# The four 32-sample strips of a scan group, one after another or side by side

## The chip, the core and the metric

The kernel runs on one core of one Trainium2 chip. The metric is the device time of one execution, in microseconds (us). The engines that matter here: PE (TensorE, the matrix unit, 128 rows by 128 columns), PEld (its weight loads), DVE (VectorE), ACT (ScalarE), POOL (GpSimd) and SP (which starts the transfers of weights). Each engine works through its own list in order and waits for the others by semaphores.

## The reference, cut to what matters

One layer of a streaming encoder for 256 prompt tokens and 32 sample tokens, 288 in all. The part that changes is the state-space scan (Mamba-2 SSD): 32 heads of 64 channels in 4 groups of 8 heads, state size 128. The prompt is scanned as chunks of the sequence with a state handed on, the sample is one chunk of 32 that starts from a given state.

```python
cum = jnp.cumsum(dtc * a.reshape(B_GROUPS, B_HPG), axis=2)
seg = jnp.where(causal, cum[:, :, :, None] - cum[:, :, None, :], -jnp.inf)
cb = jnp.einsum('bclgn,bcsgn->bclsg', cc, bc)
wgt = cb[..., None] * jnp.exp(seg) * dtc[:, :, None]
y_diag = jnp.einsum('bclsgr,bcsgrp->bclgrp', wgt, x)
decay_to_end = jnp.exp(cum[:, :, -1:] - cum) * dtc
states = jnp.einsum('bclgn,bclgr,bclgrp->bcgrpn', bc, decay_to_end, x)
...
y_off = jnp.einsum('bclgn,bcgrpn,bclgr->bclgrp', cc, h_in, jnp.exp(cum))
```

## The kernel before, in words

All tokens are columns: a tile is 128 channels by 288 tokens. The bulk of the work is the projections. Each projection is cut into jobs; a job is half a strip, a weight block of 8 x 128 x 128 that SP fetches (`wr`), that ACT copies to a rounded half `wh` (L231) and DVE to the rest `wl` (L232), and that PE then uses in 24 matmuls of 288 columns into a bank called `ps` (all matmuls go through the helper at L78). `run` takes one job after another:

```python
        convert()
        go(wh, wl)
        step()
```

`convert` puts the next weight block's copies into the lists of ACT and DVE, `go` the 24 matmuls and, at the end of a strip, the copy of its result, and `step` advances the side work by one `yield`. So in every list the order of one step is: weight copy, result copy, side work. Side work is written as generators; in the scan one is active at a time (`width["n"] = 1`), and when one ends the next starts within the same `step`.

`scan(g)` is the generator of group g. It holds 4 strips of 128 channels (two heads each), and treats the tokens in three column blocks, `COLS`: 0 to 128, 128 to 256 and the 32 samples. Its results on PE go to banks called `sd`; there are five, handed out in turn:

```python
        return psum.tile([P, 512], F32, tag="sd", bufs=5, name="sd")
```

The first matmul into a bank waits until the bank's last reader, five requests earlier, is done. A group asks for 12 banks: `pc`, `pb` (products of C and B, and B transposed), three `px` (the inputs transposed), one for the first state, four for the outputs `po`, two for the later states (`pp`). The work on PE of a group, in its steps: (1) `pc` and `pb`, L914 and L916; (2) `px`, L932, twelve transposes; (3) the first state, one product of 512 columns; (4) and (5) the outputs of two strips each (`out`), where the samples' share is 32 rows by 64 columns of the array; (6) the later states: one product with all 128 rows and one with the samples' 32 rows, 512 columns each. In between DVE subtracts the decays (L950, `decay`), ACT takes exponentials, POOL and DVE multiply by the mask (`mask`, L954; for the samples L982), POOL scales by the decay to the end (L942, `ddx`) and by the whole decay (L1028), and DVE adds the new states (L1031). The samples' tiles use 32 of the 128 partitions.

`g_misc` runs once, early: it makes `dt`, the running sums `cum`, the decays `dde` and `ecE`, and writes the transposed sums to `scr` in memory, from which POOL's transfers (L906, L909) spread them over partitions for each group. The scan runs beside 32 jobs of gate projections (`N_G`), 16 of `pm` and 16 of `az`; after these 64 jobs `begin_y` empties the side work before the next projection goes on.

Of the kernel before, what the change touches and what calls it, by code (L numbers as in the profile page):

```python
# [7 lines left out]
F32 = mybir.dt.float32  # L8
F32R = mybir.dt.float32r
AF = mybir.ActivationFunctionType  # L10
OP = mybir.AluOpType
AX = mybir.AxisListType

P = 128
TP = 256
TS = 32
T = TP + TS
# [5 lines left out]
COLS = ((0, 128, 128), (128, 256, 128), (256, 288, 32))  # L23
# [10 lines left out]
def step_kernel(ctx, tc, ins, outs):  # L34
    nc = tc.nc
    V, S, G, PE = nc.vector, nc.scalar, nc.gpsimd, nc.tensor
    PS = bass.MemoryType.PSUM

    const = ctx.enter_context(tc.tile_pool(name="const", bufs=1))
# [12 lines left out]
    def sd():  # L52
        return psum.tile([P, 512], F32, tag="sd", bufs=5, name="sd")
# [23 lines left out]
    def mm(out, lhsT, rhs, start=True, stop=True):  # L77
        PE.matmul(out, lhsT, rhs, start=start, stop=stop)  # L78
# [28 lines left out]
    ident = const.tile([P, P], F32, name="ident")  # L107
# [6 lines left out]
    tri = const.tile([P, P], F32, name="tri")  # L114
# [463 lines left out]
    dt = const.tile([P, 96], F32, name="dt")  # L578
    cum = const.tile([P, 96], F32, name="cum")
    ecE = const.tile([P, 96], F32, name="ecE")  # L580
    dde = const.tile([P, 96], F32, name="dde")
    scr = dram.tile([32, T], F32, name="scr")

    def g_misc():
        yield
        p = sd()
        for i in range(3):
            PE.transpose(p[:, 64 * i:64 * i + 64], N.mi[64:128, P * i:P * i + P], ident[64:128, 64:128])
        yield
        S.activation(wt, p[:, 0:192].rearrange("p (i c) -> p i c", i=3), AF.Copy)  # L590
        yield
        u, e, z, q, a = (t2(96) for _ in range(5))
        v3 = lambda t: t.rearrange("p (i h) -> p i h", i=3)
        V.tensor_tensor(v3(u), wt[:, :, 32:64], dtb[:, None, :].to_broadcast([P, 3, 32]), OP.add)
        V.tensor_scalar(wt[:, :, 0:16], wt[:, :, 0:16], 1.0 / 32, None, OP.mult)
        for c in range(4):
            V.tensor_copy(ws[32 * c:32 * c + 32], wt[32 * c:32 * c + 32, 2, c:16:4])
        mark("misc")

        V.scalar_tensor_tensor(e, u, -1.0, u, OP.mult, OP.max)  # L600
        S.activation(e, e, AF.Exp, scale=-1.0)
        S.activation(a[:, 0:32], alog, AF.Exp)
        yield
        V.tensor_scalar(z, e, 2.0, None, OP.add)
        V.reciprocal(z, z)
        V.tensor_tensor(z, z, e, OP.mult)
        V.tensor_tensor(q, z, z, OP.mult)
        V.tensor_scalar(e, q, 1.0 / 17, None, OP.mult)
        for n in (15, 13, 11, 9, 7, 5, 3):
            V.scalar_tensor_tensor(e, e, 1.0 / n, q, OP.add, OP.mult)  # L610
        yield
        V.scalar_tensor_tensor(e, e, 1.0, z, OP.add, OP.mult)
        V.tensor_scalar(u, u, 0.0, None, OP.max)
        V.scalar_tensor_tensor(dt, e, 2.0, u, OP.mult, OP.add)
        V.scalar_tensor_tensor(v3(u), v3(dt), -1.0, a[:, None, 0:32].to_broadcast([P, 3, 32]),
                               OP.mult, OP.mult)
        yield
        p = sd()
        for i, (c0, c1, n) in enumerate(COLS):
            h = slice(32 * i, 32 * i + 32)  # L620
            mm(p[0:n, h], tri[0:n, 0:n], u[0:n, h])
            mm(p[:, 96 + 32 * i:128 + 32 * i], ones[0:n], u[0:n, h])
        yield
        V.tensor_copy(cum[:, 0:64], p[:, 0:64])
        V.tensor_copy(cum[0:32, 64:96], p[0:32, 64:96])
        V.tensor_tensor(dde[:, 0:64], p[:, 96:160], cum[:, 0:64], OP.subtract)
        V.tensor_tensor(dde[0:32, 64:96], p[0:32, 160:192], cum[0:32, 64:96], OP.subtract)
        S.activation(ecE, p[:, 96:192], AF.Exp)
        S.activation(dde[:, 0:64], dde[:, 0:64], AF.Exp)
        S.activation(dde[0:32, 64:96], dde[0:32, 64:96], AF.Exp)  # L630
        yield
        p = sd()
        for i, (c0, c1, n) in enumerate(COLS):
            PE.transpose(p[0:32, c0:c1], cum[0:n, 32 * i:32 * i + 32], ident[0:n, 0:n])
        yield
        cumT = t2(T)[0:32]
        V.tensor_copy(cumT, p[0:32, 0:T])
        G.dma_start(scr, cumT)
# [254 lines left out]
    def heads(a):  # L893
        return a.rearrange("p (h c) -> p h c", h=8)

    def scan(g):
        hs = slice(512 * g, 512 * g + 512)
        Lt, xdt, ecB, hh, xs = N.Lt, N.xdt, N.ecB, N.hh, N.xs
        B_, C_ = N.bc[:, g], N.bc[:, 4 + g]
        src = scr[0:1]  # L900

        def col(t, i, n):
            c = 32 * i + 8 * g
            return t[0:n, c:c + 8, None].to_broadcast([n, 8, 64])

        G.dma_start(Lt, bass.AP(tensor=src.tensor, offset=src.offset + 8 * g * T,  # L906
                                ap=[[0, P], [T, 8], [1, T]]))
        for e in range(2):
            G.dma_start(ecB[64 * e:64 * e + 64],  # L909
                        bass.AP(tensor=src.tensor, offset=src.offset + (8 * g + e) * T + P,  # L910
                                ap=[[0, 64], [2 * T, 4], [1, 160]]))
        pc, pb = sd(), sd()
        for i, (c0, c1, n) in enumerate(COLS):
            mm(pc[0:n, c0:c1], B_[:, c0:c1], C_[:, c0:c1])  # L914
        for i, (c0, c1, n) in enumerate(COLS):
            PE.transpose(pb[0:n, P * i:P * i + P], B_[:, c0:c1], ident)  # L916
        yield
        cbm, bt = t2(T), t2(384)
        V.tensor_tensor(cbm[:, 0:256].rearrange("p (i t) -> p i t", i=2),
                        pc[:, 0:256].rearrange("p (i t) -> p i t", i=2),  # L920
                        tri[:, None, :].to_broadcast([P, 2, P]), OP.mult)
        V.tensor_tensor(cbm[0:32, 256:288], pc[0:32, 256:288], tri[0:32, 0:32], OP.mult)
        S.activation(bt[:, 0:256], pb[:, 0:256], AF.Copy)
        S.activation(bt[0:32, 256:384], pb[0:32, 256:384], AF.Copy)
        yield

        px = []
        for i, (c0, c1, n) in enumerate(COLS):
            p = sd()
            px.append(p)  # L930
            for j in range(4):
                PE.transpose(p[0:n, P * j:P * j + P], xs[:, 4 * g + j, c0:c1], ident)  # L932
        yield

        def xd(i):
            n = COLS[i][2]
            V.tensor_tensor(heads(xdt[0:n, i]), heads(px[i][0:n]), col(dt, i, n), OP.mult)

        def ddx(i):
            n = COLS[i][2]  # L940
            d = t2()
            G.tensor_tensor(heads(d[0:n]), heads(xdt[0:n, i]), col(dde, i, n), OP.mult)  # L942
            return d


        def decay(*rs):
            for r in rs:
                for i, (c0, c1, n) in enumerate(COLS):
                    h = 32 * i + 8 * g + r
                    V.tensor_scalar(Lt[0:n, r, c0:c1], Lt[0:n, r, c0:c1], cum[0:n, h:h + 1], 0.0,  # L950
                                    OP.subtract, OP.min)

        def mask(eng, r0, r1):
            eng.tensor_tensor(Lt[:, r0:r1, 0:256], Lt[:, r0:r1, 0:256],  # L954
                              cbm[:, None, 0:256].to_broadcast([P, r1 - r0, 256]), OP.mult)
# [15 lines left out]
        S.activation(hh[:, 0, hs], p, AF.Copy)  # L971
        yield
        decay(6, 7)
        mask(G, 0, 2)
        yield
        S.activation(Lt[:, 4:8, 0:256], Lt[:, 4:8, 0:256], AF.Exp)
        S.activation(Lt[0:32, :, 256:288], Lt[0:32, :, 256:288], AF.Exp)
        mask(V, 2, 4)
        yield
        mask(V, 4, 6)  # L980
        mask(G, 6, 8)
        G.tensor_tensor(Lt[0:32, :, 256:288], Lt[0:32, :, 256:288],  # L982
                        cbm[0:32, None, 256:288].to_broadcast([32, 8, 32]), OP.mult)
        yield 2

        po = []
# [1 line left out]
        def out(*js):  # L988

            for j in js:  # L990
                po.append(sd())
            for j in js:
                for i, (c0, c1, n) in enumerate(COLS[0:2]):
                    for e in range(2):
                        r = 2 * j + e
                        mm(po[j][64 * e:64 * e + 64, c0:c1], xdt[:, i, 64 * r:64 * r + 64], Lt[:, r, c0:c1])
                for w, o, c0, c1 in ((0, 288, 128, 256), (1, 416, 256, 288)):
                    for e in range(2):
                        a = P * (4 * g + j) + 64 * e
                        mm(po[j][64 * e:64 * e + 64, o:o + c1 - c0], hh[:, w, a:a + 64], C_[:, c0:c1])  # L1000
            for j in js:
                for e in range(2):
                    r = 2 * j + e
                    mm(po[j][64 * e:64 * e + 64, 256:288], xdt[0:32, 2, 64 * r:64 * r + 64], Lt[0:32, r, 256:288])

        def put(j):
            p, s = po[j], 4 * g + j
# [11 lines left out]
        yield  # L1019
        put(2)  # L1020
        put(3)
        pp = []
        for i, n in ((1, 128), (2, 32)):
            p = sd()
            mm(p, bt[0:n, P * i:P * i + P], ds[i - 1][0:n])
            pp.append(p)
        for i, w in ((1, 0), (2, 1)):
            G.tensor_tensor(heads(hh[:, w, hs]), heads(hh[:, w, hs]), col(ecE, i, P), OP.mult)  # L1028
        yield
        for w in range(2):  # L1030
            V.tensor_tensor(hh[:, w, hs], hh[:, w, hs], pp[w], OP.add)  # L1031
        G.dma_start(outs["ssm"][:, :, hs], hh[:, :, hs])

    hook(begin_scan)
# [232 lines left out]
```

## Time and profile before

| | |
|---|---|
| median of 3 runs | 1348.78 us (1347.21 to 1349.9) |
| the profiled execution | 1347.85 us, of which 1346.1 us are the span of the trace |
| PE busy | 1328.0 us, 99% of the span |
| DVE, ACT, POOL busy | 763.2 us (57%), 624.3 us (46%), 209.0 us (16%) |
| granted clock of PE | 0.997 over the span |
| the four groups of the scan | 538.06 to 753.56 us, 53.87 us each |

A busy PE with neighbours that are not tells that an instruction added to PE costs its own time, and one added elsewhere costs only what PE waits for. In the timeline a row is a run of like instructions: start, duration from its first start to its last end, engine, line, what is written from what, rows*columns of the array in use, shape, count. Matmuls overlap, so what a group of them costs is read from one start to another, not from durations. A product in full precision shows as two records; a transpose shows as one.

### The profile page before, as it was taken

To read this page: it belongs to the slowest core of one execution; us is meant where nothing else is said; L and a number is where in the kernel's file an instruction comes from. 1 tells how busy PE (TensorE), PEld (TensorE's weight loads), DVE (VectorE), ACT (ScalarE), POOL (GpSimd) and SP (SyncE) were. 2 spreads that over 40 slices of the span, in tenths; PEclk is the share of its full clock that TensorE was granted. 3 is DMA by queue.
4 is the path that set the end of the run, shared out by engine and by line. 5 is a ranking of instruction groups with operands and counts; after the bars stand their busy time and mean duration, and the time that the engine had idled before them with its cause. 6 is when DMAs were issued, how large, how long until landed. Compare 5 with 4: busy or idle time off the path is not lost.

```text
span 1346.1 us, 24533 instructions
## 1 busy us (share of the span) xinstructions
PE 1328.0 (99%) x10102; PEld 1296.4 (96%) x10102; DVE 763.2 (57%) x1175; ACT 624.3 (46%) x871; POOL 209.0 (16%) x291
## 2 busy tenths in 40 slices
PE   9999999999999999999999999999999999999996
PEld 9889999899999999999999999999999999999995
DVE  6874434584577767646566546763344444555444
ACT  6654443444555544735435346664333434334331
POOL 0001000000012212122231234510012000000552
PEclk9999999999999999999999999999999999999998
DMA  8767343344444444655546444444446544445442
GB/s 296 259 210 259 131 141 126 130 157 171 158 142 145 154 157 165 227 168 175 186 141 193 167 163 166 160 169 172 162 169 233 172 167 172 167 164 173 169 162 100
DMA packets 64815, 232.05 MB, mean 172 GB/s; under 512 B 7552, under 2 KB 8224, under 8 KB 63424
## 3 DMA queue, kind: packets, MB, share of 16 engines
q1 hardware_dynamic: 60800, 212.25, 45.7%
q0 software_dynamic: 3328, 16.91, 3.7%
q8 instruction: 79, 1.29, 0.4%
q10 hardware_dynamic: 576, 1.34, 0.3%
q14 instruction: 32, 0.26, 0.1%
HBM read 223.06 MB, written 7.33 MB: 171 GB/s over the span
## 4 chain that ended last, share of the span: by engine, by line
PE 93%; DVE 2%; DMA 2%; issue 1%; ACT 1%; DVEq 0%; SPq 0%; ACTq 0%
PE ps L78 85%; PE sd L78 7%; DMA wr<-in_w_mk 2%; DVE wl L232 1%; ACT wh L231 1%; PE sd L932 0%; DVE A L1161 0%; DVE ev L385 0%; PE sd L798 0%; PE sd L506 0%; PE sd L916 0%; ACT t L661 0%; DVE E L346 0%; DVE t L610 0%; DVE xl L141 0%
## 5 line engine op out<-in xcount | busy, mean ns | idle before, releaser
L232 DVE TENSOR_TENSOR wl<-wr,wh 128x1024 fp32r<-128x1024 f32 (+1 forms) x395 | 487.3, 1235 | 539.9 <-ACT wh L231 530.3
L231 ACT ACTIVATE wh<-wr 128x1024 fp32r<-128x1024 f32 (+1 forms) x395 | 416.2, 1056 | 598.3 <-PE ps L78 467.1
L78 PE MATMUL ps<-xh,wh 128*128 128x288 f32 x2384 | 644.4, 298 | 0.0
L78 PE MATMUL ps<-xl,wh 128*128 128x288 f32 x2128 | 567.0, 293 | 0.2 <-DVE xl L141 0.2
L78 PEld LDWEIGHTS ps<-xh,wh 128*128 128x128 f32 x2384 | 448.7, 188 | 7.5 <-issue 5.5
L78 PEld LDWEIGHTS ps<-xl,wh 128*128 128x128 f32 x2128 | 401.4, 189 | 1.7 <-issue 0.7
L78 PE MATMUL ps<-xh,wl 128*128 128x288 f32 x2384 | 361.0, 293 | 0.0
L78 PEld LDWEIGHTS ps<-xh,wl 128*128 128x128 f32 x2384 | 327.8, 188 | 0.0
L78 PE MATMUL ps<-B,wh 128*128 128x288 f32 (+1 forms) x320 | 77.0, 291 | 0.0
L78 PE MATMUL ps<-E,wh 128*128 128x288 f32 x256 | 69.2, 298 | 0.0
L78 PE MATMUL ps<-A,wh 128*128 128x288 f32 x256 | 68.3, 294 | 0.0
L78 PE MATMUL ps<-mgl,wh 128*128 128x288 f32 x256 | 68.2, 293 | 0.0
L78 PE MATMUL ps<-F,wh 128*128 128x288 f32 x256 | 68.2, 293 | 0.0
L861 POOL COPY cso<-t 128x3 f32<-128x3 f32 x24 | 23.1, 961 | 237.8 <-ACT t L859 237.8
L78 PEld LDWEIGHTS ps<-B,wh 128*128 128x128 f32 x320 | 56.3, 189 | 0.0
L78 PEld LDWEIGHTS ps<-E,wh 128*128 128x128 f32 x256 | 48.2, 188 | 1.1 <-issue 0.8
L78 PEld LDWEIGHTS ps<-F,wh 128*128 128x128 f32 x256 | 48.3, 189 | 0.2 <-issue 0.2
L78 PEld LDWEIGHTS ps<-mgl,wh 128*128 128x128 f32 x256 | 48.3, 189 | 0.0
L78 PEld LDWEIGHTS ps<-A,wh 128*128 128x128 f32 x256 | 48.2, 188 | 0.0
L78 PE MATMUL ps<-E,wl 128*128 128x288 f32 x256 | 38.7, 293 | 0.0
L78 PE MATMUL ps<-A,wl 128*128 128x288 f32 x256 | 38.7, 293 | 0.0
L78 PEld LDWEIGHTS ps<-E,wl 128*128 128x128 f32 x256 | 35.2, 188 | 0.0
(302 smaller groups left out, 1149.1 us busy)
## 6 DMA issues: line engine op xcount, KB each, us to landing
wr<-in_w_in SPq DMA_DIRECT2D x266, 512.0 KB, 3.3
wr<-in_w_pb SPq DMA_DIRECT2D x32, 512.0 KB, 3.3
wr<-in_w_o SPq DMA_DIRECT2D x32, 512.0 KB, 3.2
wr<-in_w_mv SPq DMA_DIRECT2D x16, 512.0 KB, 4.3
wr<-in_w_pm SPq DMA_DIRECT2D x16, 512.0 KB, 3.2
wr<-in_w_pa SPq DMA_DIRECT2D x16, 512.0 KB, 3.2
wr<-in_w_mk SPq DMA_DIRECT2D x15, 512.0 KB, 5.1
B<-scr POOLq DMA_DIRECT2D x4, 1152.0 KB, 9.6
```

What stands on the lines that cost most here:

```text
L78: PE.matmul(out, lhsT, rhs, start=start, stop=stop)
L231: S.activation(wh, raw, AF.Copy)
L232: V.tensor_tensor(wl, raw, wh.bitcast(F32), OP.subtract)
L861: G.tensor_copy(cso[:, c, 0:3], u[:, 256:259])
```

## The change

The samples of the four strips move to 32 rows or columns of the array each. In step (1) the samples' `pc` and `pb` are made four times, into four groups of 32 partitions; the transposed B becomes a product with the identity. In (2) the samples' four transposes become four products with the identity, into four groups of partitions of one bank. All the elementwise work on the samples then has 128 partitions and a quarter of the columns (two heads in place of eight). In (4) and (5) strip j uses rows 32j to 32j+32 of the array. In (6) the samples' state becomes four products of 128 columns, one per strip, each with its own 32 rows and its own bank, in a step of their own; DVE adds them in four pieces. `g_misc` makes the samples' sums four times, and POOL arranges per-strip copies of `dt`, `cum` and `dde` in `smp` and of the mask in `tri4` by 16 small copies.

```diff
 def g_misc():
-            mm(p[0:n, h], tri[0:n, 0:n], u[0:n, h])
+            for a in range(0, P, n):
+                mm(p[a:a + n, h], tri[0:n, 0:n], u[0:n, h])
...
+        for j in range(4):
+            a = slice(32 * j, 32 * j + 32)
+            for i, t in enumerate((dt, cum, dde)):
+                G.tensor_copy(smp[a, i].rearrange("p (g e) -> p g e", g=4),
+                              t[a, 64:96].rearrange("p (g r) -> p g r", g=4)[:, :, 2 * j:2 * j + 2])
+            G.tensor_copy(tri4[a], tri[a, a])
...
 def scan(g):
+        Ls, xds = Lt[:, 0:2, 256:288], xdt[:, 2, 0:P]
...
+        for j in range(4):
+            G.dma_start(Ls[32 * j:32 * j + 32], bass.AP(tensor=src.tensor, offset=src.offset + (8 * g + 2 * j) * T + 256,
+                                                        ap=[[0, 32], [T, 2], [1, 32]]))
...
-        for i, (c0, c1, n) in enumerate(COLS):
-            mm(pc[0:n, c0:c1], B_[:, c0:c1], C_[:, c0:c1])
-        for i, (c0, c1, n) in enumerate(COLS):
-            PE.transpose(pb[0:n, P * i:P * i + P], B_[:, c0:c1], ident)
+        for i, (c0, c1, n) in enumerate(COLS[0:2]):
+            mm(pc[:, c0:c1], B_[:, c0:c1], C_[:, c0:c1])
+        for i, (c0, c1, n) in enumerate(COLS[0:2]):
+            PE.transpose(pb[:, P * i:P * i + P], B_[:, c0:c1], ident)
+        for a in range(0, P, 32):
+            mm(pc[a:a + 32, 256:288], B_[:, 256:288], C_[:, 256:288])
+        for a in range(0, P, 32):
+            mm(pb[a:a + 32, 256:384], B_[:, 256:288], ident)
...
-                PE.transpose(p[0:n, P * j:P * j + P], xs[:, 4 * g + j, c0:c1], ident)
+                if n == P:
+                    PE.transpose(p[:, P * j:P * j + P], xs[:, 4 * g + j, c0:c1], ident)
+                else:
+                    mm(p[32 * j:32 * j + 32, 0:P], xs[:, 4 * g + j, c0:c1], ident)
...
-                for i, (c0, c1, n) in enumerate(COLS):
+                for i, (c0, c1, n) in enumerate(COLS[0:2]):
...
+        for e in range(2):
+            V.tensor_scalar(Ls[:, e], Ls[:, e], smp[:, 1, 2 * g + e:2 * g + e + 1], 0.0, OP.subtract, OP.min)
...
-        S.activation(Lt[0:32, :, 256:288], Lt[0:32, :, 256:288], AF.Exp)
+        S.activation(Ls, Ls, AF.Exp)
...
-                    r = 2 * j + e
-                    mm(po[j][64 * e:64 * e + 64, 256:288], xdt[0:32, 2, 64 * r:64 * r + 64], Lt[0:32, r, 256:288])
+                    a = slice(32 * j, 32 * j + 32)
+                    mm(po[j][64 * e:64 * e + 64, 256:288], xds[a, 64 * e:64 * e + 64], Ls[a, e])
...
-        pp = []
-        for i, n in ((1, 128), (2, 32)):
-            p = sd()
-            mm(p, bt[0:n, P * i:P * i + P], ds[i - 1][0:n])
-            pp.append(p)
+        p = sd()
+        mm(p, bt[:, P:2 * P], ds[0])
...
-        for w in range(2):
-            V.tensor_tensor(hh[:, w, hs], hh[:, w, hs], pp[w], OP.add)
+        V.tensor_tensor(hh[:, 0, hs], hh[:, 0, hs], p, OP.add)
+        pp = [sd() for _ in range(4)]
+        for j in range(4):
+            a = slice(32 * j, 32 * j + 32)
+            mm(pp[j][:, 0:P], bt[a, 2 * P:3 * P], ds[1][a, 0:P])
+        yield
+        for j in range(4):
+            a = slice(512 * g + P * j, 512 * g + P * j + P)
+            V.tensor_tensor(hh[:, 1, a], hh[:, 1, a], pp[j][:, 0:P], OP.add)
         G.dma_start(outs["ssm"][:, :, hs], hh[:, :, hs])
```

Two places in the engines' lists, both where group 0 ends and group 1 begins. First DVE: `wl` is a weight copy and begins a step, `A<-A,sd` the addition of a state, `t<-sd,tri` the first mask of the new group. Before:

```order
L1008 SCALAR_TENSOR_TENSOR D<-D,cols,sd 128x288
L1010 TENSOR_TENSOR ev<-sd,B 128x160
L232 TENSOR_TENSOR wl<-wr,wh 128x2x512
L1031 TENSOR_TENSOR A<-A,sd 128x512 x2
L232 TENSOR_TENSOR wl<-wr,wh 128x2x512
L919 TENSOR_TENSOR t_6595<-sd,tri 128x256
L922 TENSOR_TENSOR t_6595<-sd,tri 32x32
```

and with the change:

```order
L1036 SCALAR_TENSOR_TENSOR D<-D,cols,sd 128x288
L1038 TENSOR_TENSOR ev<-sd,B 128x160
L232 TENSOR_TENSOR wl<-wr,wh 128x2x512
L1055 TENSOR_TENSOR A<-A,sd 128x512
L232 TENSOR_TENSOR wl<-wr,wh 128x2x512
L1063 TENSOR_TENSOR A<-A,sd 128x128 x4
L232 TENSOR_TENSOR wl<-wr,wh 128x2x512
L941 TENSOR_TENSOR t_6666<-sd,tri 128x256
```

The addition of the samples' states moves one step later, behind one more weight copy; it is still the step before the new group's first mask, which is the step in which the new group's PE work begins.

Second PE, in that same step, behind the 24 matmuls of a job: `sd<-G` are the products of C and B, `sd<-ident,G` the transposes of B or products with the identity. Before:

```order
L78 MATMUL ps<-xh,wl 128x288 x8
L78 MATMUL sd<-G 128x128 [waits DVE_49,PE_49]
L78 MATMUL sd<-G 128x128
L78 MATMUL sd<-G 32x32
L916 MATMUL sd<-ident,G 128x128 [waits DVE_49,PE_49]
L916 MATMUL sd<-ident,G 128x128
L916 MATMUL sd<-ident,G 32x128
```

and with the change:

```order
L78 MATMUL ps<-xh,wl 128x288 x8
L78 MATMUL sd<-G 128x128 [waits DVE_49]
L78 MATMUL sd<-G 128x128
L934 MATMUL sd<-ident,G 128x128 [waits DVE_49]
L934 MATMUL sd<-ident,G 128x128
L78 MATMUL sd<-G 32x32 x4
L78 MATMUL sd<-ident,G 32x128 x4
```

The two small products become eight, they move behind the two transposes, and the first transpose keeps a wait for DVE.

## Rows read from the trace of the kernel before

**Rows 1.** The page: busy time by engine, and the chain that ended last by engine; and from the chain in order of time one piece, three jobs of 24 matmuls (start, us, what).

```profile
PE 1328.0 (99%) x10102; PEld 1296.4 (96%) x10102; DVE 763.2 (57%) x1175; ACT 624.3 (46%) x871; POOL 209.0 (16%) x291
...
PE 93%; DVE 2%; DMA 2%; issue 1%; ACT 1%; DVEq 0%; SPq 0%; ACTq 0%
...
547.06 9.44 PE ps L78 x72
```

**Rows 2.** Busy time by stretch, a stretch for each group of the scan: length, then PE, PEld, DVE, ACT, POOL (instructions), granted clock, share and rate of the DMA engines.

```profile
538.06:591.93 53.87, 53.87 (x446) 51.17 (x445) 29.83 (x55) 29.44 (x35) 13.04 (x15) 1.00 0.56 193
...
sum 215.50, PE 215.50 PEld 204.69 DVE 128.44 ACT 102.27 POOL 54.15; mean PE 53.88 PEld 51.17 DVE 32.11 ACT 25.57 POOL 13.54
```

**Rows 3.** Timeline of PE in group 0, from several stretches: start, us, engine, line, operation, what is written, rows*columns of the array, shape, count. The `ps` rows are the first or second matmul of the next job. The row of five is the row of six seen from its second record on.

```profile
538.19 0.79 PE L78 MATMUL sd<-G 128*128 128x128 f32 x6
538.30 0.68 PE L78 MATMUL sd<-G 128*128 128x128 f32 x5
538.91 0.55 PE L916 MATMUL sd<-ident,G 128*128 128x128 f32 x3
539.43 0.29 PE L78 MATMUL ps<-xl,wh 128*128 128x288 f32 x1
545.59 1.47 PE L932 MATMUL sd<-ident,D 128*128 128x128 f32 x12
547.03 0.29 PE L78 MATMUL ps<-xl,wh 128*128 128x288 f32 x1
556.33 1.02 PE L78 MATMUL sd<-t,t 128*128 128x512 f32 x2
557.32 0.29 PE L78 MATMUL ps<-xl,wh 128*128 128x288 f32 x1
577.83 0.42 PE L78 MATMUL sd<-B 32*64 32x32 f32 x8
578.18 0.40 PE L78 MATMUL ps<-xh,wh 128*128 128x288 f32 x1
586.80 2.07 PE L78 MATMUL sd<-t,t 128*128 128x512 f32 x4
587.75 1.12 PE L78 MATMUL sd<-t,t 32*128 32x512 f32 x2
588.80 0.40 PE L78 MATMUL ps<-xh,wh 128*128 128x288 f32 x1
589.04 0.29 PE L78 MATMUL ps<-xl,wh 128*128 128x288 f32 x1
```

**Rows 4.** Timeline of PE outside the scan, where parts of the array were already used: four groups of 32 columns (128*32), two groups of 64 rows (64*128), one group of 32 rows (32*128).

```profile
461.44 0.49 PE L798 MATMUL sd<-ident,t 128*128 128x128 f32 x3
461.86 0.48 PE L78 MATMUL sd<-C,B 128*32 128x160 f32 x8
462.52 0.30 PE L78 MATMUL ps<-xl,wh 128*128 128x288 f32 x1
...
237.38 0.93 PE L78 MATMUL sd<-C,B 64*128 64x128 f32 x8
238.24 0.40 PE L78 MATMUL ps<-xh,wh 128*128 128x288 f32 x1
...
486.22 0.48 PE L78 MATMUL sd<-t,C 32*128 32x128 f32 x2
486.64 0.40 PE L78 MATMUL ps<-xh,wh 128*128 128x288 f32 x1
486.87 0.29 PE L78 MATMUL ps<-xl,wh 128*128 128x288 f32 x1
```

**Rows 5.** Timelines of PE and DVE where group 1 begins (592) and where group 3 begins (700).

```profile
592.06 0.79 PE L78 MATMUL sd<-G 128*128 128x128 f32 x6
592.31 1.23 DVE L232 TENSOR_TENSOR wl<-wr,wh 128x1024 fp32r<-128x1024 f32 x1 [2.72 <-ACT wh L231]
593.46 1.28 DVE L1031 TENSOR_TENSOR A<-A,sd 128x512 f32<-128x512 f32 x2
597.70 0.41 DVE L919 TENSOR_TENSOR t<-sd,tri 128x256 f32<-128x256 f32 x1
...
701.48 0.44 DVE L1039 TENSOR_TENSOR C<-C,ps 128x288 f32<-128x288 f32 x1
701.85 1.27 DVE L1031 TENSOR_TENSOR A<-A,sd 128x512 f32<-128x512 f32 x2
```

**Rows 6.** Timelines of DVE and PE at a place where PE waits for DVE: the square brackets hold PE's idle time and what ended it.

```profile
243.35 0.43 DVE L637 COPY t<-sd 32x288 f32<-32x288 f32 x1
243.84 0.49 PE L78 MATMUL sd<-C,B 64*128 64x128 f32 x2 [0.81 <-DVE t L637]
```

**Rows 7.** POOL: groups of small copies (busy us, mean ns; idle before), and its two transfers after `g_misc`.

```profile
L861 POOL COPY cso<-t 128x3 f32<-128x3 f32 x24 | 23.1, 961 | 237.8 <-ACT t L859 237.8
L862 POOL COPY cso<-t 128x3 f32<-128x3 f32 x24 | 4.4, 183 | 0.0
242.40 0.58 POOL L734 DMA_DIRECT2D out_attn_k<-C  x1 [80.25 <-ACT C L731]
```

**Rows 8.** The last additions of the scan on DVE, and the first result of the projection behind `begin_y` on ACT.

```profile
755.78 1.27 DVE L1031 TENSOR_TENSOR A<-A,sd 128x512 f32<-128x512 f32 x2
782.24 0.41 ACT L1079 ACTIVATE ev<-ps 128x288 f32<-128x288 f32 x1
```

More of the change, by code (lines that the diff above doesn't have):

```diff
@@ L581, in step_kernel @@
     dde = const.tile([P, 96], F32, name="dde")
+    smp = const.tile([P, 3, 8], F32, name="smp")
+    tri4 = const.tile([P, 32], F32, name="tri4")
     scr = dram.tile([32, T], F32, name="scr")
@@ L620, in g_misc @@
             h = slice(32 * i, 32 * i + 32)
-            mm(p[0:n, h], tri[0:n, 0:n], u[0:n, h])
+            for a in range(0, P, n):
+                mm(p[a:a + n, h], tri[0:n, 0:n], u[0:n, h])
             mm(p[:, 96 + 32 * i:128 + 32 * i], ones[0:n], u[0:n, h])
         yield
[L624 to L627, printed above, removed]
+        V.tensor_copy(cum, p[:, 0:96])
+        V.tensor_tensor(dde, p[:, 96:192], cum, OP.subtract)
         S.activation(ecE, p[:, 96:192], AF.Exp)
-        S.activation(dde[:, 0:64], dde[:, 0:64], AF.Exp)
-        S.activation(dde[0:32, 64:96], dde[0:32, 64:96], AF.Exp)
+        S.activation(dde, dde, AF.Exp)
+        for j in range(4):
[4 more added lines that the diff above has]
+            G.tensor_copy(tri4[a], tri[a, a])
         yield
@@ L900, in scan, with two, scol @@
         src = scr[0:1]
+        Ls, xds = Lt[:, 0:2, 256:288], xdt[:, 2, 0:P]
+        def two(a):
+            return a.rearrange("p (e c) -> p e c", e=2)
+        def scol(i, w):
+            return smp[:, i, 2 * g:2 * g + 2, None].to_broadcast([P, 2, w])
         def col(t, i, n):
@@ L904, in col @@
             return t[0:n, c:c + 8, None].to_broadcast([n, 8, 64])
-        G.dma_start(Lt, bass.AP(tensor=src.tensor, offset=src.offset + 8 * g * T,
-                                ap=[[0, P], [T, 8], [1, T]]))
+        G.dma_start(Lt[:, :, 0:256], bass.AP(tensor=src.tensor, offset=src.offset + 8 * g * T,
+                                             ap=[[0, P], [T, 8], [1, 256]]))
+        for j in range(4):
+            G.dma_start(Ls[32 * j:32 * j + 32], bass.AP(tensor=src.tensor, offset=src.offset + (8 * g + 2 * j) * T + 256,
+                                                        ap=[[0, 32], [T, 2], [1, 32]]))
         for e in range(2):
@@ L921, in scan @@
                         tri[:, None, :].to_broadcast([P, 2, P]), OP.mult)
-        V.tensor_tensor(cbm[0:32, 256:288], pc[0:32, 256:288], tri[0:32, 0:32], OP.mult)
-        S.activation(bt[:, 0:256], pb[:, 0:256], AF.Copy)
-        S.activation(bt[0:32, 256:384], pb[0:32, 256:384], AF.Copy)
+        V.tensor_tensor(cbm[:, 256:288], pc[:, 256:288], tri4, OP.mult)
+        S.activation(bt, pb[:, 0:384], AF.Copy)
         yield
@@ L931, in scan @@
             for j in range(4):
-                PE.transpose(p[0:n, P * j:P * j + P], xs[:, 4 * g + j, c0:c1], ident)
+                if n == P:
+                    PE.transpose(p[:, P * j:P * j + P], xs[:, 4 * g + j, c0:c1], ident)
+                else:
+                    mm(p[32 * j:32 * j + 32, 0:P], xs[:, 4 * g + j, c0:c1], ident)
         yield
         def xd(i):
-            n = COLS[i][2]
-            V.tensor_tensor(heads(xdt[0:n, i]), heads(px[i][0:n]), col(dt, i, n), OP.mult)
+            if i == 2:
+                V.tensor_tensor(two(xds), two(px[2][:, 0:P]), scol(0, 64), OP.mult)
+            else:
+                V.tensor_tensor(heads(xdt[:, i]), heads(px[i]), col(dt, i, P), OP.mult)
         def ddx(i):
-            n = COLS[i][2]
             d = t2()
-            G.tensor_tensor(heads(d[0:n]), heads(xdt[0:n, i]), col(dde, i, n), OP.mult)
+            if i == 2:
+                G.tensor_tensor(two(d[:, 0:P]), two(xds), scol(2, 64), OP.mult)
+            else:
+                G.tensor_tensor(heads(d), heads(xdt[:, i]), col(dde, i, P), OP.mult)
             return d
@@ L947, in decay @@
             for r in rs:
-                for i, (c0, c1, n) in enumerate(COLS):
+                for i, (c0, c1, n) in enumerate(COLS[0:2]):
                     h = 32 * i + 8 * g + r
-                    V.tensor_scalar(Lt[0:n, r, c0:c1], Lt[0:n, r, c0:c1], cum[0:n, h:h + 1], 0.0,
-                                    OP.subtract, OP.min)
+                    V.tensor_scalar(Lt[:, r, c0:c1], Lt[:, r, c0:c1], cum[:, h:h + 1], 0.0, OP.subtract, OP.min)
         def mask(eng, r0, r1):
@@ L981, in scan @@
         mask(G, 6, 8)
-        G.tensor_tensor(Lt[0:32, :, 256:288], Lt[0:32, :, 256:288],
-                        cbm[0:32, None, 256:288].to_broadcast([32, 8, 32]), OP.mult)
+        G.tensor_tensor(Ls, Ls, cbm[:, None, 256:288].to_broadcast([P, 2, 32]), OP.mult)
         yield 2
```

## The prediction, made before the changed kernel was run

> **What bounds the kernel now.** I read the page's busy times and chain first, then the stretches of the four groups, then the timelines of PE and DVE at the places that the change touches. PE is busy 99% of the span and makes 93% of the chain; DVE has 57%, ACT 46%, POOL 16% [rows 1]. In the scan it is the same: of 53.87 us of a group PE is busy 53.87, DVE 30, POOL 13, at granted clock 1.00, the 2.4 GHz level [rows 2]. The reader is to see there that no engine but PE sets the time. So I count what PE issues more or less, and every place where PE has to wait; what DVE, ACT and POOL save is worth nothing unless PE waits for it.
>
> The measure of a piece of side work on PE is the time from its first record to the second `ps` matmul behind it, since leaving it makes that second one late. A full-precision record of 128 columns takes 0.11 us from start to start (538.19 to 538.30) [rows 3], an ordinary `ps` matmul 0.13 us (72 of them 9.44, so a job 3.15) [rows 1].
>
> **PE's own work, per group.**
> Step (1), products and transposes of B. Before: 538.19 to 539.43, 1.24 us [rows 3]. After: four full records 0.44, two transposes 0.22, then the array changes to strips of 32 columns. That costs 0.09: three transposes that lead into strips take 0.42 (461.44 to 461.86) where three times 0.11 is 0.33 [rows 4]. The four products of 32 columns are not in the trace as a foursome; the least is two slots of 0.05, the most the 0.35 us that eight narrow records take (577.83 to 578.18) [rows 3]; I take 0.15, nearer the first, since four column strips run together in the next row. The four products with the identity: the same eight records with 160 columns in four strips take 461.86 to 462.52, 0.66 us, to the second `ps` [rows 4]; a record of 512 columns takes 0.43 (586.80 to 587.75 is 0.95 for two and a change of mode [rows 3]), so 32 columns less in two slots save 0.05: 0.61. Sum 1.51: plus 0.27 (0.22 to 0.47).
> Step (2). Before: 545.59 to 547.03, 1.44 us [rows 3]. After: eight transposes 0.88, the change of mode 0.09, the foursome 0.61: 1.58, plus 0.14. A transpose was one record and the product that replaces it is two, but four run side by side, so this is nearly even.
> Steps (4) and (5), outputs. The eight records of the samples take 0.35 us (577.83 to 578.18) in one group of 32 rows [rows 3]. With the two strips in different rows they can run in half the slots: minus 0.10 each, 0.20 a group (bounds 0 and 0.35).
> Step (6), later states. Before: 586.80 to 589.04, 2.24 us [rows 3]. After, the first product alone costs what the first state does, 556.33 to 557.32, 0.99 us. The samples' four products of 128 columns in 32 rows: one of them, two records, takes 486.22 to 486.87, 0.65 us [rows 4]. That four take no longer is my choice: of two halves of 64 rows the eight records, of 128 and 256 columns, take 237.38 to 238.24, 0.86 us [rows 4], where eight one after another, at the 0.21 of one in such a mode (486.22 to 486.64 is 0.42 for two), would need 1.7 at least. With 0.09 for the change of mode, and less one ordinary `ps` interval of 0.13 that this second visit contains, 0.99 + 0.74 - 0.13 = 1.60: minus 0.64. The other end is four in a row, 8 records of 0.21 in place of two slots, 1.70 for 0.42: 1.28 more, so plus 0.64.
> Sum per group: 0.27 + 0.14 - 0.20 - 0.64 = -0.43, for four groups -1.7 us. In `g_misc` three more narrow products come once, 0.1 us at most.
> The Trainium skill, TensorEngine Tiling (Array Packing), Theoretical Speedup, gives up to four times where the small dimension is 32 or less. By it the samples' state, 1.05 us for its two records of 512 columns [rows 3], would shrink to 0.26. The row shows why I do not take that: a record of 128 columns in 32 rows takes 0.21, not a quarter of 0.53, so two slots are 0.42. By the rule the four groups would save 0.6 us more.
>
> **The wait that is added.** The `sd` banks are five, handed out in turn. A group asked for 12 and now asks for 15, and its last four requests are the samples' states. So `pb`, the second request of the next group, gets the bank of the first of these, whose reader is DVE's first narrow addition. That addition stands in the same step as the new group's products, behind that step's weight copy. Before, `pb` got a bank whose reader was done a step earlier, and the additions could run late: DVE's stood at 593.46, after PE had begun the group at 592.06 [rows 5]. Now PE must stop for the first of them before the first transpose. DVE's weight copy begins at 592.31, since ACT's half of it follows PE's matmuls of that step, and the addition at 593.46. A narrow one takes 0.28 (two of 512 columns 1.28, one of 256 0.41 [rows 5], so about 0.1 per 100 columns), and PE goes on 0.06 after such an end (243.35 + 0.43 to 243.84 [rows 6]): 593.80. PE would have come to the transpose after four full records, 592.50. The wait is 1.30 us. Queued behind the transpose on PE is everything, the six products and all `ps` matmuls, and PE has no slack later to win it back.
> It comes where groups 1, 2 and 3 begin, not at group 0. With the added step, group 3 begins in the `pm` jobs, where DVE's result copy stands between the weight copy and the additions, 0.37 more (701.48 to 701.85 [rows 5]): 1.67. Together 1.30 + 1.30 + 1.67 = 4.3 us. The other two waits of this kind are covered: `pc` waits for the wide addition, a step earlier, and `px` for the other narrow ones, two steps later.
>
> **What is hidden.** POOL's four more transfers per group, about 0.6 us each to issue by the one in [rows 7], and 16 small copies stand in front of nothing that PE needs soon: the copies take 0.18 each (3 us) or, by the slowest such row, 0.96 (15 us), from about 236 us on, and POOL has nothing before 242.40 [rows 7] and no wait of PE behind it until the scan. In the second case the `scr` transfer is some 9 us later, and a score's buffer could wait 0.5 us for it. The narrower DVE, ACT and POOL work (two heads' columns in place of eight) saves on engines with slack. The added step moves the scan's end four steps later, 12.6 us; the last additions were at 755.78, and the projection behind `begin_y` has its first result at 782.24, begun two jobs earlier at about 776 [rows 8], so three steps are left.
>
> **Sum.** -1.7 + 0.1 + 4.3 = +2.7 us, on the profiled execution's 1347.85 us 1350.6. That execution was 0.93 below the median, so on the median, 1348.78, it is 1351.5 us. A measurement of this kernel can tell 0.2%, 2.7 us, from no change; the forecast lies on that edge, on the slow side.
>
> **Rivals.**
> A. The wait does not cost: the additions come in time, because PE's own work ahead of the transposes or DVE's weight copy falls otherwise than in the old timeline. For it: only 1.3 us are to be bridged, of a step of 3.15. Against it: the copy follows PE's matmuls of the same step in every row I read, so both move together. Then -1.6 remains: 1347.2 us, no change or faster.
> B. Four groups of 32 rows do not run side by side: step (6) costs 1.28 more per group, 5.1 in all, if they run one by one; 2.1 if only the weight loads queue up (0.11 of the 0.21 of a record, since 128 columns stream in 0.11: eight loads and one streaming, 0.95, for 0.42). The place is the four products of the samples' state; it decides from two groups of rows at a time on. Then 1353.6 to 1356.6, slower. For it: the trace has only two halves of 64 rows together, never four of 32. Against it: those two were as quick as one. The Trainium skill, TensorE: Matmul & The Clock Gate, Part 3, has four row tiles at 3.07 times one; by it four groups would lose about 0.5 us in all.
> C. POOL's copies are slow and hold `scr` up, or its small copies slow DVE while scores wait for it: 0.5 us, 1352.0.
>
> **How the numbers follow.** My forecast 0.70, its own range 1350.2 to 1352.8 from the bounds of steps (1), (4) and (5); A 0.12; B 0.13; C 0.05. The forecast lies about half on each side of the edge of 1351.5: 0.33 within, 0.37 slower. A gives 0.09 within and 0.03 faster, B 0.13 slower, C 0.02 within and 0.03 slower. That makes faster 0.03, same 0.44, slower 0.53. The range leaves out half of A and the far end of B: 1347.2 to 1354.6.
>
> **What would show it.** Right: where groups 1 to 3 begin, PE's transpose (L934) waits 1.2 to 1.7 us for DVE's addition (L1063), and at group 0 not; step (6)'s four products take about 0.65 to the second `ps`; from one group's first product to the next one's (14 jobs before, 15 now) the time grows by one job less 0.4, and by the wait that falls into it. Wrong: no such wait (A), eight records of the samples' state over more than 1 us (B), idle time of PE anywhere else in the scan, or DVE's weight copies later than in the old timeline.

## The result, and the profile after

The changed kernel takes 1360.28 us (median of 4 runs, 1359.63 to 1360.75), the kernel before 1347.99 us in the same series. The ratio is 1.0083, with a 95% interval of 1.0071 to 1.0095: slower by 12.3 us. The forecast was 2.7 us slower, 1351.5 us, and its range ended at 1354.6. The profiled execution of the changed kernel took 1359.63 us, its span is 1357.9 us, the granted clock 0.997 as before.

First the places that the prediction spoke of. PE's timeline in group 0 of the changed kernel, to be read against [rows 3]: start, us, engine, line, operation, what is written, rows*columns of the array, shape, count.

```profile
542.57 0.61 PE L78 MATMUL sd<-G 128*128 128x128 f32 x4
543.41 0.41 PE L78 MATMUL sd<-ident,G 128*32 128x128 f32 x8
543.98 0.30 PE L78 MATMUL ps<-xl,wh 128*128 128x288 f32 x1
...
550.20 1.03 PE L954 MATMUL sd<-ident,D 128*128 128x128 f32 x8
551.76 0.29 PE L78 MATMUL ps<-xl,wh 128*128 128x288 f32 x1
...
582.83 0.32 PE L78 MATMUL sd<-B 32*64 32x32 f32 x8
583.08 0.40 PE L78 MATMUL ps<-xh,wh 128*128 128x288 f32 x1
...
591.64 1.02 PE L78 MATMUL sd<-t,t 128*128 128x512 f32 x2
592.64 0.29 PE L78 MATMUL ps<-xl,wh 128*128 128x288 f32 x1
...
594.61 1.23 PE L78 MATMUL ps<-xh,wl 128*128 128x288 f32 x8
595.77 0.50 PE L78 MATMUL sd<-t,t 32*128 32x128 f32 x8
596.20 0.40 PE L78 MATMUL ps<-xh,wh 128*128 128x288 f32 x1
596.44 0.29 PE L78 MATMUL ps<-xl,wh 128*128 128x288 f32 x1
```

Read from start to start, as the prediction did: step (1) 542.57 to 543.98, 1.41 us; step (2) 550.20 to 551.76, 1.56; an output step's eight small records 582.83 to 583.08, 0.25 where they took 0.35; the later states 591.64 to 592.64, 1.00, and in their second visit 595.77 to 596.44, 0.67. The eight records of the samples' state, 32 rows each, are done in 0.43 us (595.77 to 596.20), two slots of the 0.21 that one such record takes [rows 4]: four groups of rows do run side by side.

Then the places where the groups begin, PE first and DVE behind it; they answer to [rows 5]. The square brackets hold idle time and what ended it.

```profile
599.48 0.61 PE L78 MATMUL sd<-G 128*128 128x128 f32 x4
601.22 0.44 PE L934 MATMUL sd<-ident,G 128*128 128x128 f32 x2 [1.13 <-DVE A L1063]
...
657.74 0.61 PE L78 MATMUL sd<-G 128*128 128x128 f32 x4
659.47 0.44 PE L934 MATMUL sd<-ident,G 128*128 128x128 f32 x2 [1.13 <-DVE A L1063]
...
715.65 0.61 PE L78 MATMUL sd<-G 128*128 128x128 f32 x4
717.75 0.44 PE L934 MATMUL sd<-ident,G 128*128 128x128 f32 x2 [1.49 <-DVE A L1063]
...
599.74 1.23 DVE L232 TENSOR_TENSOR wl<-wr,wh 128x1024 fp32r<-128x1024 f32 x1 [1.95 <-ACT wh L231]
600.88 0.88 DVE L1063 TENSOR_TENSOR A<-A,sd 128x128 f32<-128x128 f32 x4
```

Four full records take 0.44, so the transpose of group 1 could have come at 599.92 and came at 601.22, 1.30 us late. By the same reading the transpose of group 2 is 1.29 late, that of group 3 1.66. PE waits for nothing at group 0. The cause is the one that was forecast, DVE's first narrow addition behind the weight copy.

The stretches from one group's first product to the next one's, against [rows 2]: length, PE, PEld, DVE, ACT, POOL (instructions), granted clock, share and rate of the DMA engines.

```profile
542.57:599.48 56.91, 56.91 (x493) 54.44 (x491) 30.22 (x51) 30.64 (x35) 15.66 (x19) 1.00 0.56 188
599.48:657.74 58.26, 57.13 (x493) 54.47 (x492) 28.96 (x53) 30.41 (x36) 16.36 (x20) 1.00 0.52 170
```

The forecast for the first was 53.87 and a job of 3.15 less 0.4, 56.6 us; it is 56.91. The second holds the first wait. The 0.3 that is too much is the first trace of what follows: 15 jobs of 0.03 more each, 0.45, less the 0.1 by which the other steps came out better.

So the scan's own steps did what the sum says. What it does not say is seen on matmuls that the change doesn't touch. The page before and after, the busy times and four groups of unchanged `ps` matmuls (busy us, mean ns). Before:

```profile
L78 PE MATMUL ps<-xh,wh 128*128 128x288 f32 x2384 | 644.4, 298 | 0.0
L78 PE MATMUL ps<-xl,wh 128*128 128x288 f32 x2128 | 567.0, 293 | 0.2 <-DVE xl L141 0.2
L78 PE MATMUL ps<-xh,wl 128*128 128x288 f32 x2384 | 361.0, 293 | 0.0
...
L78 PE MATMUL ps<-E,wl 128*128 128x288 f32 x256 | 38.7, 293 | 0.0
```

After:

```profile
PE 1334.1 (98%) x10200; PEld 1302.5 (96%) x10200; DVE 758.1 (56%) x1161; ACT 632.1 (47%) x872; POOL 222.2 (16%) x323
...
L78 PE MATMUL ps<-xh,wh 128*128 128x288 f32 x2384 | 648.5, 299 | 0.0
L78 PE MATMUL ps<-xl,wh 128*128 128x288 f32 x2128 | 569.8, 295 | 0.2 <-DVE xl L141 0.2
L78 PE MATMUL ps<-xh,wl 128*128 128x288 f32 x2384 | 365.6, 296 | 0.0
...
L78 PE MATMUL ps<-E,wl 128*128 128x288 f32 x256 | 38.8, 293 | 0.0
```

The same number of the same matmuls is busy 4.1, 2.8 and 4.6 us longer where the streamed operand is `xh` or `xl`, and as long as before where it is `E`. DVE is no busier than in [rows 1], so it isn't more traffic of that engine; ACT and POOL are busier (632.1 and 222.2 us against 624.3 and 209.0), and whether that matters is left to the experiments. The chains of waits show the price of a job. In the changed kernel six jobs of 24 matmuls in the scan, and eight jobs behind it (start, us, what):

```profile
736.92 19.06 PE ps L78 x144
...
816.24 25.41 PE ps L78 x192
```

and six and eight such jobs in the chain of the kernel before:

```profile
557.36 18.88 PE ps L78 x144
...
807.87 25.21 PE ps L78 x192
```

Six jobs take 19.06 in place of 18.88: 3.177 us a job in place of 3.147, 1% more; eight take 25.41 in place of 25.21. Laid beside each other, the two traces drift apart by that much at every such job, ahead of the scan, in it and behind it. The table has the start of the same job in the changed kernel less that in the kernel before, each from the start of its span, worked out from the two traces (us). A job is counted here as 24 matmuls into `ps`, 374 in all. Jobs 264 to 276 stream `E` and `F`, 312 to 341 `A` and `B`:

```
job          0     48    54    132   198   264   276   312   342   372
changed    1.50   2.41  2.13  4.29  8.08  9.85  9.85 10.81 10.81 11.72
```

The first 1.50 lies ahead of the first job, where PE waits for the first transfers of weights. It differs from execution to execution: 0.32 to 1.67 in the traces of the experiments below. Between jobs 132 and 198 lies the scan. Of the 10.2 us behind the first job, 6.4 lie outside of it.

### The profile page after: what moved, and what is told of

It is laid out like the page before. It is cut to its first block, busy times and chain, and to the rows that moved or that the text cites. A ratio compares the mean times of both kernels' runs of the same rounds, so it can differ in the third digit from the quotient of the medians.

```text
span 1357.9 us, 24779 instructions
## 1 busy us (share of the span) xinstructions
PE 1334.1 (98%) x10200; PEld 1302.5 (96%) x10200; DVE 758.1 (56%) x1161; ACT 632.1 (47%) x872; POOL 222.2 (16%) x323
## 5 line engine op out<-in xcount | busy, mean ns | idle before, releaser
L78 PE MATMUL ps<-xh,wl 128*128 128x288 f32 x2384 | 365.6, 296 | 0.0
L78 PEld LDWEIGHTS ps<-xh,wl 128*128 128x128 f32 x2384 | 333.2, 188 | 0.0
```

## The experiments

**The theory and its rival.** The unchanged matmuls became slower because their operands lie elsewhere. The change allocates two constants, `smp` (96 bytes a partition) and `tri4` (128 bytes), behind `xh` and `xl` and ahead of the weights and of the work slots. So `wh` and `wl` move 224 bytes on, `E`, `F`, `A` and `B` with them, and `xh` and `xl` stay. The jobs that became slower are those whose two operands moved against each other. The rival: the changed code, by its number of instructions or its traffic, slows PE. An experiment's edit is shown first, then what was expected of it before it ran.

**The shift alone, and the shift undone.** In the kernel before, one unused tile as large as the two constants; in the changed kernel, 32 bytes more, which makes the shift 256.

```diff
     dde = const.tile([P, 96], F32, name="dde")
+    pad = const.tile([P, 56], F32, name="pad")
+    G.memset(pad, 0.0)
```

> The kernel before with one unused tile of 224 bytes per partition, filled with zeros once, allocated behind the other constants: the weights, the work slots and all that is allocated later lie 224 bytes further on, as in the changed kernel; nothing of the scan is changed. Theory 'addresses' (the unchanged ps matmuls became slower since the weights moved against xh and xl): the jobs with xh or xl as moving operand take 3.18 us in place of 3.15, the others stay, and the time is 1348 + 8.9 = about 1357 us. Rival 'code' (the changed kernel's other instructions, in their number or their traffic, slow the matmuls): 3.15 us everywhere and 1348 us.

```diff
     tri4 = const.tile([P, 32], F32, name="tri4")
+    pad = const.tile([P, 8], F32, name="pad")
+    G.memset(pad, 0.0)
```

> The changed kernel with 32 unused bytes per partition behind its new constants, so that the whole shift is 256 bytes in place of 224. Theory 'addresses', if what counts repeats every 256 bytes: jobs with xh and xl are back at 3.15 us, and 1360.3 - 8.9 = about 1351.4 us, which is the forecast's sum. Rival 'code': 3.18 us as in the changed kernel and 1360.3 us. If addresses count but not with a period of 256 bytes, the time is near 1360 too, and the kernel before with the 224 bytes tells that from 'code'.

Measured: the kernel before with 224 unused bytes takes 1356.79 us, ratio 1.0054 (1.0041 to 1.0066). The changed kernel with 32 unused bytes takes 1352.1 us, ratio 1.0015 (1.0006 to 1.0024). Its page:

```profile
PE 1327.7 (98%) x10200; PEld 1295.9 (96%) x10200; DVE 758.6 (56%) x1161; ACT 631.3 (47%) x872; POOL 222.5 (16%) x324
...
L78 PE MATMUL ps<-xh,wl 128*128 128x288 f32 x2384 | 361.0, 293 | 0.0
```

and from its chain the six and eight jobs:

```profile
733.85 18.88 PE ps L78 x144
...
812.74 25.21 PE ps L78 x192
```

The page of the kernel before with 224 bytes:

```profile
PE 1336.3 (99%) x10102; PEld 1304.5 (96%) x10102; DVE 763.2 (56%) x1175; ACT 626.1 (46%) x871; POOL 209.8 (15%) x292
...
L78 PE MATMUL ps<-xh,wl 128*128 128x288 f32 x2384 | 365.6, 296 | 0.0
```

and from its chain three jobs, 9.44 in [rows 1]:

```profile
157.49 9.53 PE ps L78 x72
```

Not one instruction of the scan is needed for the loss, and all of the changed code runs without it. PE's busy time tells it by itself: 1328.0 before, 1336.3 with the unused tile; 1334.1 changed, 1327.7 with the 32 bytes. The drift against the kernel before, counted as above:

```
job                       0     48    54    132   198   264   276   312   342   372
before, 224 bytes       0.65   1.65  1.72  3.88  5.26  7.02  7.02  7.98  7.98  8.89
changed, 32 bytes       1.67   2.42  2.13  2.13  4.87  4.87  4.87  4.87  4.87  4.87
```

By the traces the address costs 8.89 - 0.65 = 8.2 us from the first job to job 372; by the medians of that series, 1356.79 against 1349.53, it is 7.3. Once the shift is 256, nothing drifts behind job 54 but the scan. What is left there, between jobs 132 and 198, is 4.87 - 2.13 = 2.74 us. The forecast's sum for it was 4.3 - 1.7 = 2.6.

**The wait taken away.** The next group begins one step after DVE's additions, with the address mended and without.

```diff
         G.dma_start(outs["ssm"][:, :, hs], hh[:, :, hs])
+        if g < 3:
+            yield
```

> The changed kernel with the 32 bytes, and groups 1 to 3 begin one step after DVE's additions in place of in the same step. Theory (the terms of the forecast stand): without the wait of 1.3 to 1.7 us at three groups, 4.3 us less than with the 32 bytes alone: 1351.4 - 4.3 = about 1347 us, and the first transpose of groups 1 to 3 waits for nothing. Rival (PE's wait is only moved, to the later additions or to the projection behind the scan, which comes nearer by three steps): 1351.4 us or more.

> The changed kernel where groups 1 to 3 begin one step after DVE's additions, addresses as in the changed kernel. Theory: the wait is worth 4.3 us, whatever the addresses: 1360.3 - 4.3 = about 1356 us, jobs with xh still 3.18 us. Rival (the wait is hidden or taken over by another): 1360.3 us.

Measured: 1347.08 us with the 32 bytes, ratio 0.9985 (0.9976 to 0.9994), and 1355.89 us without them, ratio 1.0046 (1.0033 to 1.0058). PE at the start of group 1 in the first of the two:

```profile
601.34 0.61 PE L78 MATMUL sd<-G 128*128 128x128 f32 x4
601.78 0.38 PE L936 MATMUL sd<-ident,G 128*128 128x128 f32 x2
```

The transpose follows 0.44 behind the first record, at once. No wait of PE appears elsewhere in the scan or at the projection behind it. The scan's drift in this trace is 1.54 - 3.45 = -1.91 us, where the forecast's work alone was -1.7. Against 2.74 the waits and what hangs on them were worth 4.65 us; 4.25 of it are the three waits as read above, the rest isn't assigned. By medians it is 5.0 us with the 32 bytes and, across two series, 4.4 without. With both repairs the kernel has the lowest median here, 0.15% under the kernel before in its series; runs of one kernel lie up to 0.3% apart (1346.09 to 1349.77), so a single run of each would not tell.

**Which addresses.** Four more unused tiles in the kernel before: 256 bytes behind the constants; 224 bytes ahead of `xh`; 224 bytes between `xh` and `xl`; 32 bytes behind the constants. The first and the last are the edit shown first, with `[P, 64]` and `[P, 8]`; the second puts the tile ahead of the line `xh = high()`, the third behind it:

```diff
     xh = high()
+    pad = const.tile([P, 56], F32, name="pad")
+    G.memset(pad, 0.0)
     xl = const.tile([P, 16, T], F32R, name="xl", tag="xl")
```

> The kernel before with an unused tile of 256 bytes per partition behind the constants. Theory 'addresses with a period of 256 bytes': jobs with xh at 3.15 us, 1348 to 1349 us, as before. Rival (any unused tile there, or any shift, costs): near the 1356.8 us of the 224 bytes.

> The kernel before with the 224 unused bytes ahead of xh and xl, so that the moving operands shift with the weights and their distances stay. Theory 'distance' (the moving operand's place against the weights' decides): 3.15 us and 1348 to 1349 us. Rival 'place' (the weights' own address, 192 in place of 224 past a multiple of 256, decides): 3.18 us and about 1357 us.

> The kernel before with the 224 unused bytes between xh and xl: xl moves with the weights, xh stays. Of a job's 24 matmuls 16 have xh as moving operand and 8 xl. Theory 'distance', each pair of operands for itself: two thirds of the 8.9 us, so about 1354 to 1355 us, jobs at 3.17 us. Rivals: only xl's distance counts, 1349 us; the weights' own address counts, 1357 us.

> The kernel before with an unused tile of 32 bytes per partition behind the constants: the shift of the changed kernel modulo 256 is minus 32 bytes, this is plus 32. If 32 bytes to either side cost: 3.18 us and 1357 us. If only some distances do: 3.15 us and 1349 us. No theory here says which of the two.

Measured, with the time of a job of 24 matmuls with `xh` from the trace:

```
                          median us   ratio (95%)                 job us
256 bytes behind          1348.37     0.9996 (0.9987 to 1.0005)   3.147
224 bytes ahead of xh     1348.93     0.9998 (0.9989 to 1.0007)   3.147
224 bytes between         1361.51     1.0094 (1.0079 to 1.0109)   3.193
32 bytes behind           1360.31     1.0087 (1.0070 to 1.0104)   3.187
```

An unused tile costs nothing by itself, and the weights' own address doesn't count: with everything moved together they lie at 192 past a multiple of 256, as in the changed kernel, and the jobs take 3.147. What counts is how `xh` and `xl` lie to the weights; two shifts by 256 bytes, here and in the changed kernel, left the time as it was. Plus 32 bytes costs more (3.187) than minus 32 did (3.177). The third expectation missed. Mending the distance of `xl` alone should have left two thirds of a job's loss of 0.030 us; the loss rose to 0.046. Three jobs in the four kernels' chains, in the order of the table:

```profile
156.25 9.44 PE ps L78 x72
...
157.10 9.44 PE ps L78 x72
...
157.39 9.58 PE ps L78 x72
...
157.21 9.56 PE ps L78 x72
```

So the two streamed operands don't cost each for itself: the losses don't add up pair by pair. A job runs its three kinds of pairs in a fixed order, and how they act on each other no run here shows.

**PE alone.** The last question was whether PE's own two reads, of the streamed operand and of the weights, get in each other's way, or whether the copies that ACT and DVE write at the same time do it. The edit replaces the kernel's whole work; its main loop is:

```diff
+    for h in range(0, 256, 32):
+        for l in range(0, 256, 32):
+            p = ps()
+            for r in range(6):
+                job(p[:, 0:T], view(0, h), view(4608, l), r == 0, r == 5)
```

> Not the kernel, and none of its outputs but zeros: PE alone runs the same job of 24 matmuls (xh and wh, xl and wh, xh and wl, in the same order), 6 times for each of 64 placements of xh and xl in steps of 32 bytes against the weights; DVE, ACT and POOL are idle and the operands are zeros. Places are given as xh's and xl's distance to the weights modulo 256: before 160 and 192, changed kernel 192 and 224, plus 32 bytes 128 and 160, between xh and xl 192 and 192. Theory 'PE's own two reads' (streaming and weight load meet): 3.15, 3.18, 3.19 and 3.19 us at these four places, without any other engine at work. Rival 'other engines' (the copies that ACT and DVE write meet PE's reads, and moved with the weights): the same time, 3.15 us or less, at all 64 places.

The last matmuls of successive jobs in PE's timeline, at the place of before (160 and 192) and at that of the changed kernel (192 and 224):

```profile
898.77 1.21 PE L82 MATMUL ps<-xs,wl 128*128 128x288 f32 x8
...
911.36 1.21 PE L82 MATMUL ps<-xs,wl 128*128 128x288 f32 x8
...
1070.23 1.23 PE L82 MATMUL ps<-xs,wl 128*128 128x288 f32 x8
...
1086.12 1.23 PE L82 MATMUL ps<-xs,wl 128*128 128x288 f32 x8
```

Four jobs in 12.59 us are 3.147 each, five in 15.89 are 3.178. All 64 places, us per job (mean of four jobs, from the trace; down `xh`, across `xl`, bytes past the weights modulo 256):

```
        0     32     64     96    128    160    192    224
  0   3.154  3.173  3.166  3.153  3.170  3.187  3.153  3.186
 32   3.194  3.206  3.187  3.207  3.193  3.200  3.186  3.200
 64   3.166  3.166  3.180  3.173  3.173  3.172  3.167  3.173
 96   3.204  3.193  3.173  3.153  3.187  3.180  3.180  3.194
128   3.168  3.180  3.174  3.207  3.193  3.187  3.200  3.206
160   3.173  3.193  3.181  3.166  3.180  3.193  3.147  3.175
192   3.177  3.173  3.174  3.193  3.173  3.173  3.193  3.177
224   3.190  3.193  3.186  3.200  3.200  3.153  3.176  3.207
```

The four places that ran in whole kernels have here what they had there: 3.147, 3.177, 3.187 (128 and 160) and 3.193 (192 and 192). No other engine is at work and the operands are zeros, so the rival falls: the loss arises among PE's own reads. The map is one execution, at granted clock 1.00. The mean of the 64 is 3.18, and the place of the kernel before is the lowest of all. Which of the two reads waits inside PE, and on what, the records don't tell; that stays open.

## Why the prediction was wrong, point by point

- That PE is the bound held: it is busy 98% after, and all that was gained or lost is on PE.
- Step (1) was forecast 1.51 us and took 1.41; step (2) 1.58 and 1.56; an output step minus 0.10 and minus 0.10. The later states were forecast 1.60; they took 1.00 and 0.67, and with 0.09 for the change of mode (the last `xh,wl` starts at 594.61 + 1.23 - 0.29 = 595.55, an ordinary next one would at 595.68, the first record comes at 595.77), less 0.13, it is 1.63. The sum of a group, forecast -0.43, is -0.52.
- The added wait was forecast 1.30, 1.30 and 1.67 us and was 1.30, 1.29 and 1.66, for DVE's first narrow addition and nowhere else. Rival A falls with it: PE's work and DVE's copy did move together.
- Rival B falls: eight records in 0.43 us. One after another, at the 0.21 of [rows 4], they would take 1.7, so the four groups do run four at a time. Against the form before, two records of 512 columns in 1.05 us [rows 3], it is 2.4 times, since a record of 128 columns in 32 rows takes 0.21 and not a quarter of 0.53. The Trainium skill, TensorEngine Tiling (Array Packing), Theoretical Speedup, has up to four times: against the same narrow records one by one the trace agrees, against the wide form it was right not to take the 0.26.
- The added step was forecast to leave three steps in hand at the scan's end. Its own numbers give 2.4: the additions at 755.78 + 12.6 = 768.4, the projection at 776. So it came: the last narrow additions of DVE begin at 776.52; ACT's first result of the projection behind is at 790.44, begun two jobs earlier at about 784, 2.4 steps later. Covered, as said.
- Rival C did not come: no wait of PE for `scr`. `g_misc` became 0.3 us shorter (between jobs 48 and 54 the drift falls from 2.42 to 2.13 with the 32 bytes), where 0.1 more was forecast. It is the wait of [rows 6]: PE waited 0.81 us there for DVE, and waits 0.50 in the changed kernel with the 32 bytes, 0.47 without. The changed kernel makes `cum` and `dde` there in one DVE instruction each, where the kernel before takes two; that this is what shortens the wait isn't tested by itself. The prediction had the wait among its rows and counted no saving at it.
- The forecast's own range, 1350.2 to 1352.8, doesn't come out of the bounds that it names: as bounds of a group those of steps (1), (4) and (5) give -0.8 to +1.6 us around 1351.5, 1350.7 to 1353.1. Nothing hangs on it; the measured time lies outside of both.
- The step that failed is the first one: "an ordinary `ps` matmul 0.13 us (72 of them 9.44, so a job 3.15)". It was taken as a constant and then only PE's other work was counted. In the changed kernel such a job takes 3.177 us in place of 3.147, on about 300 jobs. The part "What is hidden" went through POOL's copies and transfers and the additional step, and never asked where the new tiles lie. No rival spoke of it either. About 8 of the 12.3 us are this, on some 7,000 matmuls that the diff doesn't name; of the rest, about 2.7 are the scan, and some 1.5 lie ahead of the first job in the profiled executions. With the addresses mended the changed kernel is at 1.0015 of before, the forecast was 2.7 of 1348.78, 1.0020, inside the interval. So the forecast of the edits was right and the forecast of the kernel wrong.

The listing had a sign of it. The kernel before gives its work slots offsets of a few bytes and `xh` eight columns that nothing uses:

```python
    SHIFT = {"A": 160, "B": 32, "E": 224, "F": 32}
...
        return const.tile([P, 4616], F32R, name="xh", tag="xh")[:, 0:4608].rearrange("p (k t) -> p k t", k=16)
```

Such offsets compute nothing, so they are presumably there for addresses; no run here takes them out. A diff that allocates between two tiles which PE reads together changes the distance that they set.

## What to carry to other kernels

Where a kernel is bound by one long stream of like instructions, price that stream too: compare first, before any edited line, the duration of an unchanged group before and after. A new tile moves what is allocated behind it; if operands that are read together lie on both sides of it, round it up to 256 bytes, which was enough here, or allocate it behind both, and if offsets without a purpose stand in the code, take them for a layout. And a producer's reader that is moved into the step in which its bank is asked for again makes a wait that can be forecast from the old timeline to a few hundredths of a microsecond, and that one `yield` removes.

## What was not expected of the hardware

The rate of the same matmuls, in the same order at the same clock, depends on the distance in memory between the streamed operand and the weights: 3.147 to 3.207 us for 24 matmuls, 1.9%, over 64 places in steps of 32 bytes; a shift of 256 bytes in place of 224 restored 3.147. The Trainium skill, SBUF — State Buffer, SBUF: two separate sides, says that on the side of the engines only the port pair shared by GpSimd and VectorE makes contention and that PE never waits for anyone. The map agrees as far as other engines go, since PE alone shows the same times. That PE's rate hangs on where its own two operands lie to each other, which the runs show, the section doesn't say. The other surprise is that it isn't a sum over pairs: with `xl` mended and `xh` not, a job took 3.193, with neither 3.177.
